# The partner-row transfers of the rotary embedding are begun by ScalarE instead of the sync engine

## The chip, the cores and the metric

The kernel runs on one core of one Trainium2 chip. The metric is the device time of one execution in microseconds (us). Engines are named as the profile names them: PE is TensorE (its matmuls; PEld its weight loads), DVE is VectorE, ACT is ScalarE, POOL is GpSimd, and SP is the sync engine, which does nothing here but start transfers (SPq is its queue).

## The reference

Two transformer blocks run one after the other on one sequence of 256 tokens with 1024 channels, all in float32. Each block has two layers. Cut to what matters here:

```
# first block, per layer
x = x + 0.5 * swiglu(rms_norm(x), w_gu, w_down)
x = x + hybrid_mixer(rms_norm(x))            # mixer1 below
x = x + 0.5 * swiglu(rms_norm(x), w_gu, w_down)

def hybrid_mixer(h):
    u, va, q, k, v, qi, ki, wi, g_a, g_b = split(h @ w_in)
    y_a = gmlp_spatial(u, va) @ w_pa
    q, k, qi, ki = rope(q), rope(k), rope(qi), rope(ki)
    # per query: the 64 keys with the highest index score, then attention on them
    score = sum_heads(relu(qi . ki) * wi);  selected = top_k(score, 64)
    y_b = attention(q, k, v, selected) @ w_pb
    return (sigmoid(g_a) * y_a + sigmoid(g_b) * y_b) @ w_out

def rope(x):            # per head; x1 and x2 are the two halves of the rotated channels
    return concat(x1 * cos - x2 * sin, x2 * cos + x1 * sin)

# second block, per layer
x = x + rms_norm(hybrid_mixer_2(rms_norm(x)))   # mixer2: gated delta rule beside dilated attention, rope on 16 of 64 channels
x = x + rms_norm(conv_glu(rms_norm(x)))
```

## The kernel before, in words

Channels lie on the 128 partitions and the 256 tokens along the free axis. A projection is computed in chunks of 128 output channels. Each chunk needs one weight slab of 128x1024, loaded from memory by SP into a tile `wraw` (four buffers). A float32 product is made of three passes on reduced-precision operands: ACT copies the slab rounded into `whi` (line 239, reported as L180), DVE subtracts to get the rest `wlo` (line 240, reported as L197), and PE then runs 24 matmuls for a chunk (`mm3`, L253). Slabs are rounded ahead, with four buffers each of `whi` and `wlo`. The sums land in three PSUM banks with the tag `mm`; small products use five banks with the tag `sm`.

Rotary embedding of a chunk is `rotated` (lines 585 to 596). DVE writes the chunk times the cosines (`m1`) and times the sines (`m2`) into a tile `rm` (two buffers), which also frees the PSUM bank. The two halves of a head lie on different partitions, and engines work partition by partition, so the sine products must be moved to the partner rows: four small transfers copy row groups of `m2` to `m2s` (L593; 32 rows of 256 numbers each in mixer1, 8 rows each in mixer2). POOL then adds `m1` and `m2s`. The buffers of `rm` and `m2s` (tiles `rm2s`, two buffers, and `pm2s`, one for each chunk of a pair) come free with this addition.

In `mixer1` (lines 708 to 852, twice per execution) 12 chunks are rotated: four `qi`, four `q`, four `k`. The single index key `ki` is rotated by lines 751 to 761 in the same way: two transfers of 32 rows (`km2s`, L758), an addition on DVE, and a third transfer that copies the 64 rows of `ki` to the other 64 partitions (L761), because the score matmuls (L686) use both halves. DVE then finds the 64 best keys by eight rounds of `max` and `match_replace` for each of two query blocks (L697, L699), while PE goes on with `va`, `v`, `q` and `k`. After the last `k` chunk the attention starts: scores (L615), exponentials on ACT (tile `as`), a scaling on POOL, transposes on PE (L638). Between these steps PE works through the gate projections in a fixed order (`pump`, with the amounts in `FILL1`).

In `mixer2` (lines 859 to 1071, twice per execution) four pairs of chunks are rotated (`Q`, `K`, `K`, `Q` in the order string), eight transfers for a pair. They lie beside the delta rule, whose triangular inverse (`inverse`, lines 1218 to 1310) is a serial chain of six levels: PE multiplies (L1257), DVE writes `Tf`, PE multiplies (L1267), ACT copies the result into `XTf`, PE transposes (L1276), ACT copies into `X`, and the next level begins. PE's order in mixer2 is written out by hand, with chunks of projections between the steps of the chain.

Each engine works through its instructions in order. The order is set when the program is built, by a scheduler that uses estimated durations of all instructions; inside `manual_schedule` the named engines keep the order in which the code is written. A transfer is an instruction of the engine that begins it: it waits for the data and the buffers that it needs, and what stands behind it on that engine waits with it. The transfers of the program share eight completion semaphores in turn, so that a transfer also waits for the earlier transfer on its semaphore. Before the change, all transfers of loads, partner rows and results stand on SP in one row.

Of the kernel before, what the change touches and what calls it, by code (L numbers as in the profile page):

```python
# [87 lines left out]
class Kernel:  # L88
# [496 lines left out]
    def rotated(self, pool, ps, cs, tag, swaps, m2s):  # L585

        nc = self.nc
        m = pool.tile([P, 2, T], F32, name="rm", tag="ct", bufs=2)
        m1, m2 = m[:, 0, :], m[:, 1, :]
        self.tt(m1, ps, cs[0])  # L590
        self.tt(m2, ps, cs[1])
        for to, frm, n in swaps:
            nc.sync.dma_start(m2s[to:to + n, :], m2[frm:frm + n, :])  # L593
        o = pool.tile([P, T], F32, name=tag, tag="rope", bufs=8)
        self.turned = self.tt(o, m1, m2s, OP.add, nc.gpsimd)
        return o
# [111 lines left out]
    def mixer1(self, l, vec):  # L708
        nc, I = self.nc, self.I
# [17 lines left out]
        with mp as mp:  # L727
# [26 lines left out]
            m2 = mp.tile([64, T], F32, name="km2")  # L754
            self.tt(m2, ps[:64, :], cs[1][:64, :])
            m2s = mp.tile([64, T], F32, name="km2s")
            for to, frm, n in swaps[:2]:
                nc.sync.dma_start(m2s[to:to + n, :], m2[frm:frm + n, :])  # L758
            ki = mp.tile([P, T], F32, name="ki")
            self.tt(ki[:64, :], m1, m2s, OP.add)  # L760
            nc.sync.dma_start(ki[64:, :], ki[:64, :])  # L761
            wi = mp.tile([72, T], F32, name="wi")
            self.tt(wi[64:, :], ps[64:, :], rb[64:72, :])
            ps = self.bank([P, 2, 8], "sm")
# [18 lines left out]
            for b, ps in enumerate(self.token_layout(I["w_in_va"][l], hs)):  # L783
# [8 lines left out]
                n = gv  # L792
# [739 lines left out]
```

## Time and profile before

| what | us |
|---|---|
| three runs, lowest / median / highest | 1924.41 / 1927.37 / 1934.48 |
| the profiled execution: its own time | 1928.9 |
| its span in the trace | 1927.2 |
| PE busy | 1857.0 (96%) |
| DVE busy | 1344.8 (70%) |
| ACT busy | 992.5 (51%) |
| POOL busy | 328.5 (17%) |

Busy time does not include instructions that begin transfers, so the table says nothing of what SP does. The share of busy time is a mean over stages with different limits. PE is idle for 70.2 us of the span, and most of that lies in the two mixers. A mixer1 starts at about 200 and at about 760 us, a mixer2 at about 1135 and at about 1560 us.

### The profile page before, as it was taken

The page shows a single profiled execution, that of the slowest core. Times are in us where ns is not written, and L with a number is a line of the kernel's source. Part 1 is how long each engine was busy: PE and PEld are TensorE (multiplying, and loading weights), DVE is VectorE, ACT ScalarE, POOL GpSimd, SP SyncE. Part 2 cuts the span into 40 slices and gives each one's busy share as a digit, 9 for nine tenths or more (in the row PEclk, how much of TensorE's full clock was granted, in tenths as well). Part 3 has the DMA queues.
Part 4 walks back from the last instruction along what each step waited for, and adds up shares of the span by engine and source line. Part 5 has one row for each costly group of instructions (what it writes and reads, how often), then busy time and mean ns, then how long its engine had stood idle before and what let it go on. Part 6 is the DMA issues. An engine that isn't in the chain of part 4 may idle for free. (4 is left out here: it accounts for less than half of the span.)

```text
span 1927.2 us, 38950 instructions
## 1 busy us (share of the span) xinstructions
PE 1857.0 (96%) x15468; PEld 1801.7 (93%) x15468; DVE 1344.8 (70%) x2318; ACT 992.5 (51%) x1698; POOL 328.5 (17%) x332
## 2 busy tenths in 40 slices
PE   9999989999999999999999998988999998989998
PEld 8999989999999999889999998968999998779998
DVE  6665696876656665886866659555997586558973
ACT  5444436554444544446544545535775564356762
POOL 1001131100010001220100123223231233132311
PEclk8999999999999999999999999999999999999999
DMA  7666654666666666564666653213566543135663
GB/s 232 187 182 185 205 153 149 192 188 186 183 189 191 192 186 204 164 188 130 205 192 186 181 167 123 95 59 102 186 196 185 156 132 98 57 115 168 197 185 108
DMA packets 102503, 317.10 MB, mean 165 GB/s; under 512 B 13361, under 2 KB 20913, under 8 KB 102321
## 3 DMA queue, kind: packets, MB, share of 16 engines
q1 hardware_dynamic: 102320, 314.61, 53.3%
q8 instruction: 121, 1.98, 0.4%
q14 instruction: 62, 0.50, 0.1%
HBM read 309.58 MB, written 1.05 MB: 161 GB/s over the span
## 5 line engine op out<-in xcount | busy, mean ns | idle before, releaser
L253 PE MATMUL mm<-h,whi 128*128 128x256 f32 x6048 | 1078.4, 281 | 17.2 <-DVE rm L197 8.4
L197 DVE TENSOR_TENSOR wlo<-wraw,whi 128x1024 fp32r<-128x1024 f32 (+2 forms) x611 | 716.2, 1174 | 357.9 <-ACT whi L180 355.8
L253 PEld LDWEIGHTS mm<-h,whi 128*128 128x128 f32 x6048 | 931.0, 190 | 24.3 <-ACT h L180 7.1
L180 ACT ACTIVATE whi<-wraw 128x1024 fp32r<-128x1024 f32 (+2 forms) x611 | 614.8, 1008 | 626.3 <-issue 286.5
L253 PE MATMUL mm<-h,wlo 128*128 128x256 f32 (+1 forms) x3024 | 728.3, 281 | 8.2 <-DVE wlo L197 8.0
L253 PEld LDWEIGHTS mm<-h,wlo 128*128 128x128 f32 (+1 forms) x3024 | 573.2, 190 | 11.0 <-DVE wlo L197 9.8
L253 PE MATMUL mm<-hid,whi 128*128 128x256 f32 x2112 | 374.1, 279 | 0.0
L253 PEld LDWEIGHTS mm<-hid,whi 128*128 128x128 f32 x2112 | 322.9, 188 | 0.0
L253 PE MATMUL mm<-hid,wlo 128*128 128x256 f32 x1056 | 255.1, 279 | 0.0
L253 PEld LDWEIGHTS mm<-hid,wlo 128*128 128x128 f32 x1056 | 198.1, 188 | 0.0
L197 POOL TENSOR_TENSOR ssum<-sq 128x256 f32<-128x256 f32 x19 | 23.4, 1232 | 674.2 <-ACT sq L180 674.2
L197 DVE TENSOR_TENSOR t<-mm,rb 128x512 f32<-128x512 f32 x132 | 90.7, 688 | 16.1 <-PE mm L253 7.7
L197 POOL TENSOR_TENSOR hid<-p,hid 128x256 fp32r<-128x256 f32 x44 | 63.9, 1453 | 179.6 <-ACT hid L180 149.8
L200 DVE SCALAR_TENSOR_TENSOR y<-t,vec,y 128x255 f32<-128x255 f32 (+1 forms) x176 | 91.7, 574 | 0.0
L197 POOL TENSOR_TENSOR ssum<-ssum,sq 128x256 f32<-128x256 f32 x50 | 54.9, 1097 | 204.2 <-ACT sq L180 178.8
L180 ACT ACTIVATE hid<-p 128x256 fp32r<-128x256 f32 x132 | 53.1, 402 | 5.7 <-DVE p L197 5.5
L180 ACT ACTIVATE y<-t,vec 128x256 f32<-128x256 f32 x88 | 47.7, 592 | 9.0 <-DVE t L197 8.8
L253 PE MATMUL mm<-zh,whi 128*128 128x256 f32 x256 | 45.4, 280 | 1.7 <-ACT zh L180 1.7
L200 DVE SCALAR_TENSOR_TENSOR h<-x,vec,h 128x256 fp32r<-128x256 f32 x72 | 41.1, 579 | 6.0 <-ACT h L180 5.1
L197 POOL TENSOR_TENSOR as<-as,ast 128x512 f32<-128x512 f32 (+1 forms) x32 | 26.1, 829 | 93.6 <-DVE ast L627 80.0
L253 PEld LDWEIGHTS mm<-zh,whi 128*128 128x128 f32 x256 | 39.0, 188 | 2.5 <-ACT zh L180 2.5
L573 PE MATMUL mm<-whi,h 128*128 128x512 f32 x96 | 39.6, 412 | 0.0
(294 smaller groups left out, 1899.2 us busy)
## 6 DMA issues: line engine op xcount, KB each, us to landing
wraw<-ffn_gu_in SPq DMA_DIRECT2D x175, 512.0 KB
wraw<-w_in_a_in SPq DMA_DIRECT2D x112, 512.0 KB
wraw<-up_in SPq DMA_DIRECT2D x88, 512.0 KB
wraw<-ffn_down_in SPq DMA_DIRECT2D x64, 512.0 KB
wraw<-down_in SPq DMA_DIRECT2D x32, 512.0 KB
wraw<-ffn_down_in SPq DMA_DIRECT2D x32, 384.0 KB
wraw<-w_in_v_in SPq DMA_DIRECT2D x16, 512.0 KB
wraw<-w_out_in SPq DMA_DIRECT2D x16, 512.0 KB
```

The lines of the kernel that those rows point to most:

```text
L180: return self.nc.scalar.activation(out, in_, func, **k)
L197: return (eng or self.nc.vector).tensor_tensor(out, a, b, op=op)
L200: return self.nc.vector.scalar_tensor_tensor(out, a, s, b, op0=op0, op1=op1)
L253: mm = lambda a, b, **f: self.nc.tensor.matmul(ps, a, b, skip_group_check=shared, **f)
L573: mm(ps[b], hs[k][:, 0, t], hi[:, w], start=k == 0, stop=False)
```

## The change

Three calls in two functions begin their transfer on ACT (`nc.scalar`) instead of SP (`nc.sync`). Data, shapes, buffers and arithmetic stay as they are.

```
 def rotated(self, pool, ps, cs, tag, swaps, m2s):
         for to, frm, n in swaps:
-            nc.sync.dma_start(m2s[to:to + n, :], m2[frm:frm + n, :])
+            nc.scalar.dma_start(m2s[to:to + n, :], m2[frm:frm + n, :])
...
 def mixer1(self, l, vec):
             for to, frm, n in swaps[:2]:
-                nc.sync.dma_start(m2s[to:to + n, :], m2[frm:frm + n, :])
+                nc.scalar.dma_start(m2s[to:to + n, :], m2[frm:frm + n, :])
             ki = mp.tile([P, T], F32, name="ki")
             self.tt(ki[:64, :], m1, m2s, OP.add)
-            nc.sync.dma_start(ki[64:, :], ki[:64, :])
+            nc.scalar.dma_start(ki[64:, :], ki[:64, :])
```

This moves 166 transfers: 2 x 48 `rm2s`, 2 x 2 `km2s` and 2 x 1 `ki` in mixer1, and 2 x 32 `pm2s` in mixer2. Since the scheduler sees other durations, it also orders other instructions anew in the mixers. Three places follow. A row is a run of like instructions, with its count behind an x.

ACT in the first mixer1, from the first rounding after `rb` (the row factors of the norm) to the first `rl` (rectified index scores); `gu` is a GELU of a `u` chunk. Before:

```order
L180 ACTIVATE whi<-wraw 128x1024 x4
L180 ACT_TABLE_LOAD
L180 ACTIVATE gu<-ut 128x256 x2
L180 ACTIVATE whi<-wraw 128x1024
L180 ACTIVATE gu<-ut 128x256
L180 ACTIVATE rl<-sm 128x2x128
L180 ACTIVATE whi<-wraw 128x1024 x2
```

With the change:

```order
L180 ACTIVATE whi<-wraw 128x1024
L593 DMA rm2s<-rm 32x256 x8
L180 ACTIVATE whi<-wraw 128x1024 x2
L593 DMA rm2s<-rm 32x256 x4
L758 DMA km2s<-km_2712 32x256
L593 DMA rm2s<-rm 32x256 x4
L758 DMA km2s<-km_2712 32x256
L180 ACT_TABLE_LOAD
L180 ACTIVATE gu<-ut 128x256 x2
L180 ACTIVATE whi<-wraw 128x1024 x4
L180 ACTIVATE gu<-ut 128x256
L761 DMA ki<-ki 64x256
```

Eighteen small transfers now stand among the roundings, and the copy of `ki` stands behind four roundings and three GELUs.

ACT in the first mixer1, from the last `ya` (the high part of a gMLP output) to the first exponentials of the attention (`as`). Before:

```order
L180 ACTIVATE ya<-gm_3221 128x256
L180 ACTIVATE whi<-wraw 128x1024 x5
L180 ACT_TABLE_LOAD
L180 ACTIVATE as,ast<-as,ast 128x256 x4
L180 ACTIVATE whi<-wraw 128x1024 x2
```

With the change:

```order
L180 ACTIVATE ya<-gm_3221 128x256
L593 DMA rm2s<-rm 32x256 x6
L180 ACTIVATE whi<-wraw 128x1024 x2
L593 DMA rm2s<-rm 32x256 x4
L180 ACTIVATE whi<-wraw 128x1024
L593 DMA rm2s<-rm 32x256 x8
L180 ACTIVATE whi<-wraw 128x1024 x2
L593 DMA rm2s<-rm 32x256 x4
L180 ACT_TABLE_LOAD
L180 ACTIVATE as,ast<-as,ast 128x256 x2
L180 ACTIVATE whi<-wraw 128x1024 x2
L180 ACTIVATE as,ast<-as,ast 128x256 x2
```

The same five roundings stand ahead of the table load, with 22 transfers among them; the last four, those of the last `k` chunk, stand directly ahead of the table load, and two roundings now split the four exponentials.

ACT in the first mixer2, from the last `vT` chunk's SiLU to level 1 of the inverse, as the difference (with `vec` for the taps of the convolution, `qT` a chunk of the delta rule's queries):

```order
-L180 ACTIVATE whi<-wraw 128x1024 x3
-L180 ACTIVATE XTf<-sm 64x4x64 x4
-L180 ACTIVATE whi<-wraw 128x1024
+L180 ACTIVATE whi<-wraw 128x1024
+L593 DMA pm2s_14549<-rm 8x256 x4
+L593 DMA pm2s_14551<-rm 8x256 x4
+L593 DMA pm2s_14549<-rm 8x256 x4
+L593 DMA pm2s_14551<-rm 8x256 x4
 L180 ACTIVATE XTf<-sm 64x4x64 x4
 L180 ACTIVATE qT<-ct,vec_2412 128x256 x2
+L180 ACTIVATE whi<-wraw 128x1024 x2
```

The sixteen transfers of the first `Q` pair and the first `K` pair now stand in one row ahead of the four `XTf` copies of level 0, and two roundings moved behind these. A third burst of eight (the second `K` pair) stands directly ahead of the four `XTf` copies of level 3, and a fourth (the second `Q` pair) ahead of the squares of the first delta output.

## Rows read from the trace of the kernel before

**Rows 1.** The page, part 1: busy time, share of the span, instructions.

```profile
PE 1857.0 (96%) x15468; PEld 1801.7 (93%) x15468; DVE 1344.8 (70%) x2318; ACT 992.5 (51%) x1698; POOL 328.5 (17%) x332
```

**Rows 2.** Busy time by stretch: mixer1's parts (830: second layer), then mixer2.

```profile
core 0: us, PE busy (x) PEld busy (x) DVE busy (x) ACT busy (x) POOL busy (x), PEclk, DMA share, GB/s
205.00:228.00 23.00, 23.00 (x196) 22.59 (x195) 11.93 (x24) 8.25 (x10) 4.44 (x6) 1.00 0.51 171
228.00:262.00 34.00, 32.36 (x183) 26.61 (x181) 31.77 (x64) 16.78 (x24) 7.65 (x6) 1.00 0.59 186
262.00:293.00 31.00, 26.80 (x216) 26.21 (x216) 28.20 (x62) 10.71 (x13) 9.08 (x10) 0.94 0.59 185
830.00:862.00 32.00, 27.78 (x235) 26.47 (x235) 26.66 (x67) 15.53 (x30) 9.73 (x12) 1.00 0.64 200
1190.00:1262.00 72.00, 64.58 (x559) 61.22 (x557) 44.09 (x93) 33.37 (x79) 20.14 (x24) 0.95 0.23 73
```

**Rows 3.** Waits of PE, 200 to 300: us in total, times, longest.

```profile
PE mm L253 <- DVE rm L197: 4.2, 2, 2.6
```

**Rows 4.** The tile rm2s: transfer instructions, duration in ns min/median/max.

```profile
L593 SPq DMA_DIRECT2D rm2s<-rm x96: 507/588/1567, 210.5 to 851.4; - x96
```

**Rows 5.** SP in order of time: start, us, operation; the q and k chunks.

```profile
266.48 2.43 SPq L593 DMA_DIRECT2D rm2s<-rm  x4
...
278.70 1.47 SPq L215 DMA_DIRECT2D wraw<-w_in_a_in  x3
280.27 6.36 SPq L593 DMA_DIRECT2D rm2s<-rm  x8
```

**Rows 6.** POOL and PE in order of time, k chunks (idle before, releaser).

```profile
287.01 0.72 POOL L197 TENSOR_TENSOR k<-rm,rm2s 128x256 f32<-128x256 f32 x1 [6.32 <-DMA rm2s<-rm]
...
288.67 0.36 PE L253 MATMUL mm<-h,whi 128*128 128x256 f32 x1 [2.64 <-DVE rm L197]
```

**Rows 7.** SP, then PE: the last km2s, the copy of ki and its first use.

```profile
222.64 0.59 SPq L758 DMA_DIRECT2D km2s<-km  x1
...
225.18 0.52 SPq L761 DMA_DIRECT2D ki<-ki  x1
...
226.98 0.71 PE L686 MATMUL sm<-ki,qi 64*128 64x128 f32 x4
```

**Rows 8.** ACT in order of time, both ends of the q and k chunks.

```profile
265.37 0.42 ACT L180 ACTIVATE ya<-gm 128x256 fp32r<-128x256 f32 x1 [2.12 <-DVE gm L197]
...
294.54 1.07 ACT L180 ACTIVATE whi<-wraw 128x1024 fp32r<-128x1024 f32 x1 [7.27 <-PE mm L253]
295.62 1.28 ACT L180 ACT_TABLE_LOAD   x1
296.92 0.51 ACT L180 ACTIVATE as<-as,ast 128x256 f32<-128x256 f32 x1
```

**Rows 9.** POOL, then PE: first scaled probabilities, first transposes; first scores.

```profile
298.29 2.04 POOL L197 TENSOR_TENSOR as<-as,ast 128x512 f32<-128x512 f32 x2 [2.57 <-DVE ast L627]
...
300.12 0.60 PE L638 MATMUL sm<-ident,as 128*128 128x128 f32 x4
```

**Rows 10.** SP, ACT, PE in mixer2: bursts beside levels 0, 1 and 3.

```profile
1207.16 5.41 SPq L593 DMA_DIRECT2D pm2s<-rm  x8
...
1226.02 5.41 SPq L593 DMA_DIRECT2D pm2s<-rm  x8
...
1207.06 0.78 ACT L180 ACTIVATE XTf<-sm 64x256 f32<-64x256 f32 x2 [1.84 <-PE sm L1269]
...
1225.94 1.06 ACT L180 ACTIVATE whi<-wraw 128x1024 fp32r<-128x1024 f32 x1
1230.42 1.69 ACT L180 ACTIVATE XTf<-sm 64x256 f32<-64x256 f32 x4 [3.42 <-PE sm L1267]
...
1213.15 1.95 PE L1267 MATMUL sm<-XTf,Tf 128*128 128x128 f32 x16
...
1231.66 1.16 PE L1276 MATMUL sm<-ident,XTf 128*128 128x128 f32 x8
```

More of the change, by code (lines that the diff above doesn't have):

```diff
@@ L592, in rotated @@
         for to, frm, n in swaps:
-            nc.sync.dma_start(m2s[to:to + n, :], m2[frm:frm + n, :])
+            nc.scalar.dma_start(m2s[to:to + n, :], m2[frm:frm + n, :])
         o = pool.tile([P, T], F32, name=tag, tag="rope", bufs=8)
@@ L757, in mixer1 @@
             for to, frm, n in swaps[:2]:
-                nc.sync.dma_start(m2s[to:to + n, :], m2[frm:frm + n, :])
+                nc.scalar.dma_start(m2s[to:to + n, :], m2[frm:frm + n, :])
             ki = mp.tile([P, T], F32, name="ki")
             self.tt(ki[:64, :], m1, m2s, OP.add)
-            nc.sync.dma_start(ki[64:, :], ki[:64, :])
+            nc.scalar.dma_start(ki[64:, :], ki[:64, :])
             wi = mp.tile([72, T], F32, name="wi")
```

## The prediction

> **What bounds the kernel now.** The page's busy times come first: PE is busy 1857.0 of 1927.2 us [rows 1]. A change that touches no matmul can give back only PE's idle time, and it costs what it adds to that. So the question is where PE idles near the moved transfers, and for whom it waits there. The view of busy time by stretch answers the first part [rows 2]. In mixer1 PE has no gap while the qi chunks are rotated (205 to 228), 1.6 us in the top-k stretch (228 to 262) and 4.2 us in the stretch of the q and k chunks (262 to 293; again 4.2 in the second layer). In these last two stretches DVE is nearly full too, 31.8 of 34 and 28.2 of 31 us, while ACT is busy for 16.8 and 10.7. In mixer2, 1190 to 1262, PE idles 7.4 us.
>
> The list of PE's waits says for whom: in the first mixer1, 4.2 us go to DVE's `rm` [rows 3], the instruction that frees a PSUM bank. `rm` is late because its two buffers come free only when POOL has added the partner rows. The rows of SP and POOL show it: the first k chunk's transfers are begun at 280.27, right behind three weight slabs, and POOL can add only at 287.01, after 6.32 us of idleness put down to these transfers; PE stands for 2.64 us until 288.67 [rows 5, 6]. So the small transfers do sit on PE's path there, but only there.
>
> **The price of a transfer on ACT.** A transfer keeps SP's queue 588 ns (median; 507 at least) [rows 4], and four take 2.43 us, 0.61 each with the gaps [rows 5]. No row shows ACT beginning one. From above I take SP's 0.61 with nothing beside it; from below, zero, since an activation that runs may cover an instruction that only begins a transfer. I take 0.61, because it is the same instruction, but let the first one or two of a burst run under the activation ahead of them. Each mixer1 moves 48 + 2 + 1 = 51 transfers, 31 us of ACT's queue, and each mixer2 moves 32, 19.5 us. Whatever stands behind one on ACT waits also for what the transfer waits for: DVE's `rm`, POOL's freeing of the buffer, and the earlier transfer on its semaphore.
>
> **Part a, the qi chunks and ki (each mixer1).** SP began the copy of ki at 225.18, and PE used it at 226.98, 1.8 us later [rows 7]. With the change the copy stands on ACT behind 18 transfers, a table load, four roundings and three GELUs. The last transfer before the table load, a `km2s`, was begun by SP from 222.64 to 223.23 [rows 7]; I assume the same on ACT. Then the load 1.28, two GELUs 0.8, four roundings 4 x 1.0, a third GELU 0.4: ki's copy begins at about 229.8 and can be used at 231.6, against 226.98. In its new order PE has about one more chunk ahead of these scores, 24 matmuls at 23.00 / 196 = 0.117 us, 2.8 us [rows 2], so until about 230; it stands some 1.5 us. The first va rounding moves back with the same row of instructions; I put that at 1 us for PE, 2.5 together. A stretch follows in which DVE sets the pace, and a PE that arrives late there idles less. I take half, +1.2; bounds 0 and +2.5.
>
> **Part b, the q and k chunks (each mixer1).** The gain: SP no longer holds weights back behind `rm`, and the small transfers no longer queue behind slabs on SP's queue. At most it is the 4.2 us of idle PE, and in the first layer another 31 x 0.06 = 1.9 us of granted clock lost (0.94 there, 1.00 in the second) [rows 2]. But DVE, 28.2 of 31 us busy, leaves 2.8 us before it is the limit itself. The cost: ACT's 10.7 busy us and 32 x 0.61 = 19.5 make 30.2 of 31. ACT goes from an idle engine to a full one; if its waits for `rm` come on top, roundings are late. By SP's price and with nothing overlapped I bound that at +2.0. I take -2; bounds -4.2 (-6.1 in the first layer) and +2.0.
>
> **Part c, the start of attention (each mixer1).** ACT's last rounding before it began at 294.54 after a wait for PE; table load and exponentials follow at 295.62 and 296.92 [rows 8]. With the change the last k chunk's four transfers stand between: 4 x 0.61 = 2.4 us, 1.4 if they begin under the rounding. The first half of POOL's scaling ended at about 299.3, PE's transposes began at 300.12 [rows 9]: 0.8 us of slack. So 0.6 to 1.6 us reach PE; I take +0.8, bounds 0 and +1.6.
>
> **Part d, the inverse in mixer2 (each mixer2).** Three bursts stand directly ahead of copies that the chain needs or its squares. The first K pair's burst ran on SP from 1207.16 for 5.41 us, to 1212.6. On ACT the four `XTf` copies of level 0 come behind it: 4 x 0.39 = 1.6, done at 1214.1 instead of 1207.84. PE needs them at 1213.15 [rows 10], so +0.9. The second K pair's burst, 1226.02 to 1231.4 on SP, delays `XTf` of level 3 from 1230.42 to 1231.4, +1.0 (2.0 if it begins only when the rounding has ended at 1227.0); PE's transposes at 1231.66 move with it. The fourth burst delays squares of the first half's output by about 1.1 us; the second half ends later anyway, so I count 0.3. The first Q pair's burst is covered by the wait for level 0. Sum +2.2; bounds 0 and +4.0 by these rows, and 5.4 + 5.4 + 1.1 = 11.9 if the bursts land in full on the chain. Nothing comes back here: none of PE's waits in mixer2 ends on a `pm2s` transfer.
>
> **The sum.** Each mixer1: 1.2 - 2 + 0.8 = 0. Each mixer2: +2.2. Against the profiled execution's 1928.9 us (1927.2 of span, and 1.5 above the median of 1927.37) the forecast is 1928.9 + 2 x 0 + 2 x 2.2 = 1933.3 us, own range 1924 to 1943.
>
> **The rivals.** *ACT is held (slower).* ACT begins one transfer at a time, nothing of it under an activation. Then a, b and c stand at their upper bounds, 2.5 + 2.0 + 1.6 = 6.1 in each mixer1, and d at 4.0: 1928.9 + 2 x 10.1 = 1949.1. It decides from the point at which ACT's price reaches SP's 0.59 without overlap. For it: ACT would be full in the q and k stretch. Against it: ACT idled 7.27 us just before 294.54 [rows 8].
>
> *The small transfers get through (faster).* Taken out of SP's queue, they land soon after they begin, as the copy of ki did in 1.8 us [rows 7], instead of some 4 to 6 us when slabs stand ahead [rows 5, 6]. Then all of PE's waits on `rm` go, and ACT hides the rest: -4.2 in each mixer1 and -1.9 of clock, nothing else: 1928.9 - 10.3 = 1918.6. For it: rows 5 and 6. Against it: DVE is the next limit. The Trainium skill, "DMA: Bandwidth & Descriptors", section "Queues, rings and completion order", supports it: SP and ACT each own a row of rings, and each DMA engine takes turns between the rows that have work.
>
> *The weights do not come free (the change does not do what it says).* The semaphores still go round over both queues, so that SP's loads wait for earlier small transfers which ACT has not begun, and these share the DMA engines with slabs as before. Then b is 0 and the rest stays: 1928.9 + 2 x 2.0 + 2 x 2.2 = 1937.3. For it: the second k chunk's transfers took longer to begin than the usual 2.43 for four (eight took 6.36 us [rows 5]), so such waits exist already. The Trainium skill speaks for it too, in the same page's section "Issuing engines are not separate DMA queues": transfers from all engines run on the same 16 DMA engines, and issuing from several saves only the issuing time. By that rule alone the time would be 1937.3. Rows 6 do not tell the two apart, since all transfers of this trace come from SP.
>
> **How the numbers follow.** Chances: forecast 0.50, ACT held 0.24, transfers get through 0.10, weights not free 0.16. The range 1920 to 1949 leaves out about half of the slower rival and most of the faster one, some 0.19 in all. What a measurement can tell from no change is about 0.5%, 9.6 us: faster means below 1917.7, slower above 1937.0. Faster: nearly half of the second rival and a little of the forecast's low side, 0.06. Slower: nearly all of the first rival, half of the third and 0.05 of the forecast, 0.36. Same: 0.58.
>
> **What would show it.** In the changed trace: the transfers of `rm2s` on ACT's queue near 0.6 us each; PE's waits on `rm` in the q and k stretches down from 4.2 us; a PE wait before the index scores (L686) of 1 to 3 us; `XTf` of levels 0 and 3 starting right behind a burst. The forecast is wrong if ACT's price is far from 0.6, if PE's idle time in mixer2 grows by more than 4 us a layer, or if stretches without moved transfers change.

## The result and the profile after

The changed kernel takes 1940.04 us (median of 19 runs, 1932.66 to 1949.94) against 1926.12 us before (19 runs of the same series, 1916.65 to 1935.96). The ratio is 1.0070, 95% interval 1.0057 to 1.0084: 11 to 16 us slower, beyond the 0.5% that a measurement tells from no change. The prediction was 1933.3 in a range from 1920 to 1949, with 0.58 on "same". By its own bounds (slower above 1937.0) the outcome is "slower", to which it gave 0.36.

The profiled execution of after has a span of 1942.5 us. Its lines that answer to the rows of before are these. First the busy times [rows 1]:

```profile
PE 1867.2 (96%) x15468; PEld 1808.4 (93%) x15468; DVE 1341.7 (69%) x2318; ACT 991.3 (51%) x1698; POOL 337.8 (17%) x332
```

Next, from the list of PE's waits over the whole span (us in total, times, longest), the lines that the change bears on:

```profile
PE sm L1267 <- ACT XTf L180: 8.3, 2, 4.4
PE mm L253 <- DVE rm L197: 7.6, 9, 1.7
...
PE sm L686 <- DVE ki L197: 3.6, 2, 2.2
...
PE sm L1276 <- ACT XTf L180: 1.8, 3, 0.8
```

The waits on `rm`, which the change could have removed, are still there: 4.8 of these 7.6 us lie in the first mixer1 (3.8 in the stretch of the q and k chunks, 1.0 new among the qi chunks), against 4.2 before, all of them in the q and k chunks [rows 3]. The other three lines show PE waiting for ACT's copies in mixer2 (L1267, L1276) and for `ki` in mixer1 (L686).

Then line 593, the transfers themselves (duration in ns min/median/max), and who waited for them (us, times). It answers to [rows 4]:

```profile
L593 ACTq DMA_DIRECT2D rm2s<-rm x96: 514/602/1400, 208.2 to 853.5; - x96
...
L593 ACTq DMA_DIRECT2D pm2s<-rm x64: 631/632/1182, 1198.5 to 1674.5; - x64
...
  POOL qi L197: 35.6, 6
  ACT whi L180: 29.9, 7
  POOL rope L197: 27.2, 12
```

A transfer costs ACT what it cost SP, 0.6 us. New is the second waiter: ACT's own roundings, 29.9 us.

**Where the 13.9 us lie.** A stage is counted from the write of its row factor `rb` to the next one's. The experiments below leave one mixer or the other as it was, so that their profiles give several executions of each stage with its old code, and chance can be told from effect. For mixer2's first layer the three changed stages (205.7 to 206.5) touch the longest of the seven old ones.

| stage length, us | old code, mean (range) | all on ACT, mean | difference |
|---|---|---|---|
| mixer1, start to PE's first attention transposes (both layers) | 90.9 (89.1 to 93.1; 14 stages) | 93.4 (6 stages) | +2.5 |
| mixer2, first layer | 202.7 (200.8 to 205.8; 7) | 206.1 (3) | +3.4 |
| mixer2, second layer | 196.6 (196.0 to 197.2; 7) | 203.0 (3) | +6.4 |

The sum is 2 x 2.5 + 3.4 + 6.4 = 14.8 us, within the measured 11 to 16. So the loss is in mixer1 and mixer2, where transfers were moved.

### The profile page after: what moved, and what is told of

Its sections match the earlier page's. It is cut to its first block, busy times and chain, and to the rows that moved or that the text cites. A ratio compares the mean times of both kernels' runs of the same rounds, so it can differ in the third digit from the quotient of the medians.

```text
span 1942.5 us, 38929 instructions
## 1 busy us (share of the span) xinstructions
PE 1867.2 (96%) x15468; PEld 1808.4 (93%) x15468; DVE 1341.7 (69%) x2318; ACT 991.3 (51%) x1698; POOL 337.8 (17%) x332
## 3 DMA queue, kind: packets, MB, share of 16 engines
q1 hardware_dynamic: 96336, 310.67, 52.2%
## 5 line engine op out<-in xcount | busy, mean ns | idle before, releaser
L197 DVE TENSOR_TENSOR t<-mm,rb 128x512 f32<-128x512 f32 x132 | 90.6, 687 | 14.4 <-PE mm L253 7.5
L197 POOL TENSOR_TENSOR hid<-p,hid 128x256 fp32r<-128x256 f32 x44 | 62.1, 1410 | 184.2 <-ACT hid L180 155.4
L197 POOL TENSOR_TENSOR ssum<-ssum,sq 128x256 f32<-128x256 f32 x50 | 54.9, 1098 | 203.7 <-ACT sq L180 178.2
L180 ACT ACTIVATE XTf<-sm 64x256 f32<-64x256 f32 (+1 forms) x48 | 17.3, 360 | 58.0 <-DMA pm2s<-rm 26.0
L197 DVE TENSOR_TENSOR rm<-mm,cosr 128x256 f32<-128x256 f32 x40 | 16.6, 419 | 39.2 <-POOL qi L197 10.8
```

Source lines behind the costliest of these rows:

```text
L180: return self.nc.scalar.activation(out, in_, func, **k)
L197: return (eng or self.nc.vector).tensor_tensor(out, a, b, op=op)
```

## The experiments

Each timed kernel ran in turns with the kernel before. "Before" in the ratios is that kernel on the same chips.

**One mixer at a time.** The helper gets the queue as an argument; mixer1 passes ACT and mixer2 SP, or the other way round.

```diff
-            nc.scalar.dma_start(m2s[to:to + n, :], m2[frm:frm + n, :])
+            queue.dma_start(m2s[to:to + n, :], m2[frm:frm + n, :])
```

> Only mixer1's transfers (rm2s, km2s and the copy of ki) are begun by ACT; mixer2's pm2s stay on SP. The changed kernel is 13.9 us slower than the kernel before (1940.0 against 1926.1). Theory 'held copies': most of the loss sits in mixer2, where ACT's XTf copies stand behind K bursts; mixer1 costs 1.7 us a layer (PE's first transposes of attention come 1.7 us late in both layers of the changed trace), so 1926.1 + 3.4 = 1929.5, and mixer2's stages last as before. Rival 'price by number': every transfer on ACT costs the same, 13.9 us / 166 transfers = 0.084 us; 102 of them are here, so 1934.7. Rival 'slow matmuls': the 4.9 us that the first conv_glu lost in the changed trace, where PE did 215 matmuls in 25 us instead of 223, come from the moved transfers too, in whichever mixer; then this kernel's conv_glu also runs at 215.

Measured: 1934.12 us (12 runs), ratio 1.0043 (1.0021 to 1.0064), 4 to 12 us.

> Only mixer2's pm2s transfers are begun by ACT; mixer1's stay on SP. Theory 'held copies': 3.0 to 6.1 us a layer, as the two layers of the changed trace show, so 1926.1 + 9 = 1935 (1932 to 1938), with PE's wait before L1267 on XTf of 4 us a layer and its wait before L1276 of 0.8. Rival 'price by number': 64 x 0.084 = 5.4 us, 1931.5. Both mixers' losses should add up to 13.9 if nothing couples them.

Measured: 1937.83 us (10 runs), ratio 1.0062 (1.0035 to 1.0088), 7 to 17 us, with PE's wait before L1267 on `XTf` at 4.7 us in the first layer. Both halves lose. Their medians add up to more than 13.9, but their intervals include a pair that adds up to it. Mixer1 costs more than the 3.4 us expected; the price by number fits it (8.3 against 8.5) but not mixer2 (11.9 against 5.4). The next runs separate places from numbers.

**The two halves of mixer1.** First only the q and k chunks on ACT, then only qi, `km2s` and `ki`:

```diff
-                    out.append(self.rotated(mp, chunk(i0 + i), cs, tag, swaps, m2s))
+                    out.append(self.rotated(mp, chunk(i0 + i), cs, tag, swaps, m2s, nc.scalar if i0 else nc.sync))
```

> Only the transfers of mixer1's q and k chunks (L593 in the second call of rope_chunks) are begun by ACT; qi, km2s, the copy of ki and mixer2's pm2s stay on SP. Theory 'held copies': the wait of PE before L686 on ki is gone; what is left is the start of attention (+0.7 us a layer) against a gain of 0.6 to 1 us a layer in the stretch before it, so 1925 to 1927. The prediction's term b (-2 a layer) with term c (+0.8): 1926.1 - 2.4 = 1923.7. Rival 'price by number': 64 x 0.084 = +5.4, 1931.5.

Measured: 1934.18 us, 1.0030 (1.0008 to 1.0052), above the theory's 1925 to 1927, while its two mixer1 stages were 0.45 us shorter and 0.53 longer than in the first profile of before. Its two conv_glu stages, which no edit touches, were 5.0 and 3.8 us longer. So it was run again:

> The kernel with only the q and k chunks on ACT, once more: it was timed at 1.0030 (1.0008 to 1.0052), while its mixer1 stages took as long as before and its conv_glu stages, whose code is the same, 5.0 and 3.9 us longer. If the loss is in conv_glu by chance (two equal kernels differ there too), this time comes out within 0.2% of before, 1925 to 1930. If the transfers themselves cost 5.8 us, 1933 to 1935 again, with the loss in mixer1.

Measured: 1926.49 us, 1.0008 (0.9983 to 1.0033); mixer1 +0.30 and +0.53 us. The 64 transfers of q and k bring nothing. What they cost is small: about half a us at most shows in a mixer1 stage, and what both series allow is 2 to 6 us over the execution (1.0008 to 1.0033).

> The other half of mixer1: qi's transfers, km2s and the copy of ki are begun by ACT; the q and k chunks and mixer2 stay on SP. From the traces so far, PE's first transposes of attention stand 90.9 us after the start of mixer1 in 14 stages whose mixer1 is that of before (89.1 to 93.1), 93.1 in four stages with all of it on ACT, and 91.1 in two with only q and k on ACT. Theory 'late ki': this half carries the loss of mixer1, 2.2 to 2.5 us a layer, so PE reads ki first 20.2 to 21.2 us after the stage's start instead of 18.6, and the time is 1927 + 4.7 = 1931.7. Rival 'price by number': 38 transfers, 3.2 us, 1930; and the wait on ki would not matter. Rival 'given back' (DVE sets the pace of the stretch that follows): 1927.

Measured: 1934.28 us, 1.0044 (1.0026 to 1.0063), with PE's first read of `ki` 20.8 and 20.5 us after the start of mixer1 (18.5 to 18.8 where SP begins the transfers). The 38 transfers of this half carry as much as the whole of mixer1 (1.0043); "price by number" and "given back" fall. Its last step takes `km2s` and `ki` off ACT again and leaves qi there:

```diff
             for to, frm, n in swaps[:2]:
-                nc.scalar.dma_start(m2s[to:to + n, :], m2[frm:frm + n, :])
+                nc.sync.dma_start(m2s[to:to + n, :], m2[frm:frm + n, :])
...
-            nc.scalar.dma_start(ki[64:, :], ki[:64, :])
+            nc.sync.dma_start(ki[64:, :], ki[:64, :])
```

> Only the qi chunks' 16 transfers a layer are begun by ACT; km2s and the copy of ki are back on SP, where they now stand between va's weight slabs. Theory 'late ki because its km2s and its copy stand behind qi's burst on ACT': PE reads ki first 18.6 us after the stage's start again, the cost goes: 1926 to 1928. Rival 'roundings are late behind qi's burst' (the first transposes of wi stood 1 us later in the changed trace already): 1 to 2 us a layer stay, 1929 to 1931, with ki read at 19.6 or later.

Measured: 1927.82 us, 1.0013 (0.9994 to 1.0031). SP's row of `km2s` and PE's first scores in the first layer, whose mixer1 starts at 205.49:

```profile
215.90 1.46 SPq L758 DMA_DIRECT2D km2s<-km  x2
...
223.15 0.71 PE L686 MATMUL sm<-ki,qi 64*128 64x128 f32 x4
```

Both `km2s` transfers are begun from 10.4 us after the start of the stage on, where SP's second one came after 14.4 us before and ACT's after 16.6, and `ki` is read after 17.7 us, before even the kernel before. Most of the time is back: 1.0013 against 1.0044. So `km2s` and the copy of `ki` behind qi's transfers on ACT cost the larger part. But a rest of 1 to 2 us a layer, as the rival said, shows in the trace and is within the interval, though `ki` is early: PE's first transposes of `wi` are 0.5 to 0.9 us late, its last matmuls on `ws` and `gv` (the gMLP's spatial product, which closes this stretch) come 54.2 and 53.8 us after the start (54.4 and 54.1 with `ki` on ACT too, 51.7 to 53.0 with the old code), and the first attention transposes after 93.6 and 90.9. What this rest is was not tested; qi's transfers on ACT are what is left of the change there.

**The two kinds of pair in mixer2.** Only the Q pairs on ACT, then only the K pairs (mixer1 on SP in both):

```diff
-                        out.append(self.rotated(mp, ps[:, s, :], cs, "rope", swaps, m2s[s]))
+                        out.append(self.rotated(mp, ps[:, s, :], cs, "rope", swaps, m2s[s], nc.scalar if out is q else nc.sync))
```

> In mixer2 only the Q pairs' transfers are begun by ACT; K pairs and all of mixer1 stay on SP. Theory 'burst in front of copies': a burst costs PE only where XTf or X copies that the inverse needs next stand behind it; the Q bursts have free time behind them (the first Q burst cost nothing at level 0 when the K burst was moved away), so 0 to 1 us a layer, 1926 to 1930, and mixer2's stages within 1 us of before. Rival 'late landing': the Q pair's rows land some 5 us after they are begun because SP's slabs run freely, POOL's addition and what stands behind it on POOL are late, and the cost stays at 2 us or more a layer. Rival 'price by number': 32 x 0.19 = 6 us, from the 11.9 us that 64 transfers in mixer2 cost.

Measured: 1928.47 us, 1.0001 (0.9978 to 1.0024).

> In mixer2 only the K pairs' transfers are begun by ACT; Q pairs and all of mixer1 stay on SP. In its order three of level 0's eight XTf copies more than before stand ahead of the first K burst, the other five behind it. Theory 'burst in front of copies': the burst starts when it started on SP in the kernel before (its rm is ready then, because the Q pair lands early again) and is over 5.4 us later, just before PE needs the copies; by the working of the prediction +0.9 or less for the first and +1.0 for the second, 1.0 to 2.0 us a layer, 1928 to 1930. Rival 'the K burst by itself': 4 to 6 us a layer as with all of mixer2's transfers on ACT, 1935 to 1938; the first Q pair's landing would then be without a part in it.

Measured: 1936.86 us, 1.0057 (1.0035 to 1.0078). The same number of transfers, 32 each, costs nothing in one place and about 11 us in the other: "price by number" falls in mixer2 too. The K pairs carry the loss, and more of it than the 1 to 2 us a layer of the prediction's working. The profile shows less than the median: it is that of the fastest of the ten runs (1930.45 us), and its mixer2 stages are 2.9 and 3.9 us longer than the means with the old code.

**The same number in another place.** The K pairs' transfers and additions are kept back and written behind the `XTf` copies of the level at which they fall:

```diff
+        if held is None:
+            partner()
+        else:
+            held.append(partner)
...
                 for b in range(2):
                     step(lev, b)
+                while i == 1 and k.held:
+                    with k.tc.issue_after(self.copied.ins):
+                        k.held.pop(0)()
                 k.pump(WAIT["lev%d" % i])
```

> As the kernel with only mixer2's transfers on ACT, but each K pair's transfers and POOL's additions behind them are written after the XTf copies of the inverse's level (0 and 3) that they stood in front of. Same number of transfers on ACT. Theory 'held copies': PE's wait on XTf before the first L1267 goes, and the cost falls from 9 us to 2 (1926 to 1929). Rival 'price by number' and rival 'late landing' (the transfers land late because SP's weight slabs are no longer held back behind them, and whoever needs the rotated chunks is late): nothing comes back, within 2 us of the kernel with mixer2's transfers on ACT.

Measured: 1945.26 us, 1.0100 (1.0065 to 1.0134): slower still, against the theory's 1926 to 1929. Its trace says why. ACT's rows in the first layer, then PE's row behind them:

```profile
1205.95 1.59 ACT L180 ACTIVATE XTf<-sm 64x256 f32<-64x256 f32 x4 [9.22 <-DMA pm2s<-rm]
1207.71 5.41 ACTq L596 DMA_DIRECT2D pm2s<-rm  x8
...
1233.36 4.85 ACTq L596 DMA_DIRECT2D pm2s<-rm  x7
1238.31 1.56 ACT L180 ACTIVATE X<-sm 64x256 f32<-64x256 f32 x4 [5.08 <-DMA pm2s<-rm]
...
1239.13 3.67 PE L1265 MATMUL sm<-X,LT 128*128 128x64 f32 x16 [3.93 <-ACT X L180]
```

The first burst now starts behind level 0's copies. At level 2 PE is 1.2 and 1.8 us late in the two layers, counted from the start of the stage against the mean of the seven stages with the old code, instead of 4.4 and 4.8 with the burst ahead of the copies. The second burst, moved from before the `XTf` copies of level 3 to behind them, now stands before that level's `X` copies, and its 5 us hold PE for 3.93. By the end of the inverse the layers are 7.8 and 8.4 us late. So the theory was right on the first burst and too narrow: the `X` copies, which the inverse needs next, cost as `XTf` did. "Price by number" falls, and so does "late landing" as the only cause, since with the same number of transfers each layer gained 3 us at the first burst's new place and lost 5.6 more at the second's.

**Weights held back again.** One more small transfer per chunk on SP, into a tile nobody reads, where SP's transfers stood before:

```diff
+        if extra is not None:
+            to, frm, n = swaps[0]
+            self.nc.sync.dma_start(extra[to:to + n, :], m2[frm:frm + n, :])
         for to, frm, n in swaps:
             queue.dma_start(m2s[to:to + n, :], m2[frm:frm + n, :])
```

> As the kernel with mixer2's transfers on ACT, with one more small transfer per rotated chunk on SP, into a tile that nobody reads, at the place where SP's transfers stood before. It holds SP's next weight slab back until rm is there, as before; ACT's burst is unchanged. Theory 'late landing': the first Q pair lands 2 us after it is begun instead of 5, POOL adds earlier, the K burst ends earlier, PE's wait for XTf before the first L1267 falls from 4.7 to under 2 us, and the time from 1937.8 to 1932 or less. Rival 'the K burst by itself': PE's waits stay, 1936 to 1940.

Measured: 1939.01 us, 1.0061 (1.0036 to 1.0086), as without the extra transfers. POOL's rows at the first Q pair, and PE's at level 1:

```profile
1190.17 0.73 POOL L197 TENSOR_TENSOR dM<-levels,cM 128x256 f32<-128x256 f32 x1 [6.21 <-DVE Tf L197]
1190.86 0.74 POOL L197 TENSOR_TENSOR rope<-rm,pm2s 128x256 f32<-128x256 f32 x1
...
1200.31 3.78 PE L1271 MATMUL sm<-XTf,Tf 128*128 128x128 f32 x16 [4.00 <-ACT XTf L180]
```

POOL no longer waits for the landing; it adds as soon as it gets there. But in this kernel's order it gets there late, behind a `dM` that waits for DVE. So this is no clean test of what the landing cost; it shows that early landing alone does not give the time back, because the K burst in front of the copies then ends no earlier (64.1 and 62.1 us after the start of the stage, against 63.2 and 61.7 without the extra transfers).

**Controls.** The kernel before and the changed kernel once more:

> The kernel before, unchanged, as a measure of what two equal kernels differ by, and for a second profile of it. Expected: ratio 1.000 within 0.002. In the kernel before's first profile both conv_glu stages ran at 223 matmuls in 25 us and took 193.6 and 183.8 us; in other profiles one or both took some 4 to 5 us more. If the matmul rate is a matter of the execution, this profile may show either; if it is a matter of the moved transfers, both stages take 193.6 and 183.8 again.

Measured: 1925.26 us, 0.9994 (0.9971 to 1.0016).

> The changed kernel, for a second profile. If the first conv_glu's loss of 4.9 us comes with the change, it shows again; if the matmul rate is a matter of the execution, either 193 or 198 us. Mixer1 1.5 to 3 us longer than before in each layer and mixer2 3 to 6, in either case.

Measured: one time of 1941.76 us; mixer1 2.6 and 2.7, mixer2 2.2 and 6.0 us longer than in the first profile of before; first conv_glu 193.2 us. The 4.9 us that this stage lost in the first profile of after do not come with the change; that also answers the rival "slow matmuls".

No run kept the transfers on SP and changed only the order of the other instructions, which the scheduler makes anew with every edit. What the new order alone costs is not known.

## Why the prediction came out as it did

The sign of the forecast was right and the size was a third of it: +4.4 us forecast, +13.9 measured, between the third rival's 1937.3 and the first's 1949.1. That the time lies in the stated range is no merit of the working: the range reached up to the slowest rival. By the stage averages, over both layers, a came out 2.8 us above its term, b 3.0 above, c 1.0 below and d 5.4 above; the sum of 10.2 is near the 9.5 us between the changes forecast and measured. By its own steps:

**The price, right.** 0.61 us a transfer was taken; the medians are 602 and 632 ns. That the first of a burst runs under the activation ahead was right too, and understated, as the copy of `ki` below shows.

**Part a (+1.2), mis-sized: +2.6 a layer, just above its upper bound.** Counted from the start of the stage, PE's last matmul on `ws` and `gv` (the end of the stretch that a speaks of) comes after 54.9 us on average against 52.2 with the old code. In two of the six changed stages the granted clock fell to its lower level, 1.2 GHz, shortly behind the wait on `ki` (0.97 on average over the stretch, 1.00 in the others); the other four come at 54.4. The rows of the first layer, in the order SP, ACT, POOL, DVE, PE:

```profile
209.64 18.84 SPq L215 DMA_DIRECT2D wraw<-w_in_va_in  x4
...
208.19 5.18 ACTq L593 DMA_DIRECT2D rm2s<-rm  x8
213.47 2.01 ACT L180 ACTIVATE whi<-wraw 128x1024 fp32r<-128x1024 f32 x2 [5.45 <-DMA rm2s<-rm]
...
222.60 0.60 ACTq L758 DMA_DIRECT2D km2s<-km  x1
...
227.02 0.52 ACTq L761 DMA_DIRECT2D ki<-ki  x1
...
214.45 1.43 POOL L197 TENSOR_TENSOR qi<-rm,rm2s 128x256 f32<-128x256 f32 x2 [9.27 <-DMA rm2s<-rm]
...
215.22 0.42 DVE L197 TENSOR_TENSOR rm<-mm,cosr 128x256 f32<-128x256 f32 x1 [5.60 <-POOL qi L197]
...
226.02 0.97 DVE L197 TENSOR_TENSOR ki<-km,km2s 64x256 f32<-64x256 f32 x1 [0.54 <-DMA km2s<-km]
...
216.12 0.35 PE L253 MATMUL mm<-h,whi 128*128 128x256 f32 x1 [0.99 <-DVE rm L197]
...
227.13 0.68 PE L686 MATMUL sm<-ki,qi 64*128 64x128 f32 x4 [2.18 <-DVE ki L197]
```

Before, DVE's addition for `ki`, and PE's only longer wait of this stretch (us in total, times, longest):

```profile
224.60 0.44 DVE L197 TENSOR_TENSOR ki<-km,km2s 64x256 f32<-64x256 f32 x1 [0.62 <-DMA km2s<-km]
...
PE sm L806 <- POOL gv L197: 1.5, 1, 1.5
```

This mixer1 starts at 205.98, that of before at 208.29. Counted from there, the first qi transfer begins at 2.2 us in both. But SP, whose slabs for va stood behind all of these transfers before, now starts them from 209.64 on, and POOL can add only at 8.5, after 9.27 us of idleness that ends on the transfers; before it added at 6.1. That the slabs delay the landing fits these rows; no run held them back in mixer1. DVE needs that buffer for the third chunk's `rm` (5.60 us of idleness, and 0.99 for PE behind it), and the last `km2s` goes out at 16.6 instead of 14.4 [rows 7]. It also lands later: DVE's addition follows 3.4 us after it is begun instead of 2.0, and takes 0.97 us instead of 0.44. So `ki` is ready after 21.0 us instead of 16.8, and PE reads it after 21.2 instead of 18.7. The step that failed is "I assume the same on ACT" for the last `km2s`: the clock time is nearly the same, 222.60, but the stage started 2.3 us earlier. The copy of `ki`, on which the working turned, was not what PE waited for: the first scores read the half that DVE writes. The copy went out at 227.02, 2.8 us earlier than predicted, although two roundings and a GELU stand ahead of it in ACT's order (two of the roundings began at 227.05): ACT's queue runs ahead of its engine here. Of what this stretch was to give back, PE's wait of 1.5 us on `gv` before the last matmuls is gone; against the two new waits, 0.99 and 2.18 us, that was not half.

**Part b (-2), wrong: -0.5 at most.** From that matmul to the first attention scores PE takes 30.6 us instead of 31.1, and 31.0 with the q and k chunks alone on ACT. SP is free, and its weights run on in one unbroken row, but POOL waits for the k chunks' rows as before [rows 5, 6]:

```profile
240.38 57.31 SPq L215 DMA_DIRECT2D wraw<-w_in_a_in  x17
...
287.32 0.72 POOL L197 TENSOR_TENSOR k<-rm,rm2s 128x256 f32<-128x256 f32 x1 [3.69 <-DMA rm2s<-rm]
291.68 0.72 POOL L197 TENSOR_TENSOR k<-rm,rm2s 128x256 f32<-128x256 f32 x1 [3.64 <-DMA rm2s<-rm]
```

One wait of 6.32 us has become two of 3.7, and PE's stall on `rm` several short ones. That is nearly the third rival's "b is 0". The rows fit the second of its two reasons, that the small transfers share the DMA engines with slabs, which nothing holds back any more; no run held the slabs back in this stretch. The Trainium skill, "DMA: Bandwidth & Descriptors", section "Issuing engines are not separate DMA queues", says that transfers from all engines run on the same 16 DMA engines and that issuing from several saves only the issuing time; the rows of the q and k chunks agree, with 1.0030 and 1.0008 for that part alone. The forecast left this reason at 0.16 because the trace of before could not show it. The faster rival falls by the same rows.

**Part c (+0.8), right in sign and smaller.** From PE's first attention scores to its first transposes there are 7.6 us in the 14 stages with old code and 7.5 to 8.2 in the six with all transfers on ACT, 7.9 on average: +0.3.

**Part d (+2.2), mis-sized: +3.4 and +6.4.** ACT, POOL and PE in the first layer:

```profile
1198.47 14.61 ACTq L593 DMA_DIRECT2D pm2s<-rm  x16
1213.13 1.58 ACT L180 ACTIVATE XTf<-sm 64x256 f32<-64x256 f32 x4 [15.11 <-DVE ct L197]
1214.74 0.91 ACT L180 ACTIVATE qT<-ct,vec 128x256 f32<-128x256 f32 x2
1215.56 1.99 ACT L180 ACTIVATE whi<-wraw 128x1024 fp32r<-128x1024 f32 x2
1217.57 1.59 ACT L180 ACTIVATE XTf<-sm 64x256 f32<-64x256 f32 x4
...
1229.67 5.58 ACTq L593 DMA_DIRECT2D pm2s<-rm  x8
1235.35 1.58 ACT L180 ACTIVATE XTf<-sm 64x256 f32<-64x256 f32 x4 [4.78 <-DMA pm2s<-rm]
...
1206.07 0.74 POOL L197 TENSOR_TENSOR rope<-rm,pm2s 128x256 f32<-128x256 f32 x1 [7.86 <-DMA pm2s<-rm]
...
1213.97 3.78 PE L1267 MATMUL sm<-XTf,Tf 128*128 128x128 f32 x16 [4.43 <-ACT XTf L180]
1218.62 1.54 PE L1276 MATMUL sm<-ident,XTf 128*128 128x128 f32 x8
...
1236.18 1.46 PE L1276 MATMUL sm<-ident,XTf 128*128 128x128 f32 x8 [0.80 <-ACT XTf L180]
```

Then PE's wait and the matmuls behind it, as busy time by stretch (us, then PE, PEld, DVE, ACT, POOL with counts, granted clock, DMA share, GB/s):

```profile
1209.50:1213.97 4.47, 0.04 (x2) 0.01 (x1) 2.45 (x6) 0.79 (x3) 2.13 (x3) 0.87 0.06 13
1213.97:1217.75 3.78, 3.78 (x17) 3.78 (x18) 2.47 (x5) 3.71 (x7) 0.73 (x1) 0.50 0.00 0
```

For the second K burst the working holds: +1.0 forecast, PE's wait is 0.80 and its delay grows by 1.0 in both layers. For the first the end of level 0's copies was well forecast (1214.1; 1214.7, in a stage that starts 1.0 later), though the sixteen transfers take 14.61 us instead of 16 x 0.63 = 10.1: POOL waits 7.86 us for the first Q pair's rows. Against the mean of the seven stages with the old code PE's L1267 starts 1.5 us late in the first layer and 2.1 in the second. What the working left out comes next: PE had idled for 4.43 us, the granted clock fell to 0.50, its lower level of 1.2 GHz, and the same 16 matmuls took 3.78 us instead of 1.95 [rows 10]. This is so in all six stages with mixer2's transfers on ACT: a wait of 3.2 to 4.7 us, then 3.2 to 3.8 us for these matmuls, against 1.95 to 2.04 in the 14 stages with the old code. At level 1's L1276 PE is therefore 3.7 and 4.2 us late. ACT's queue does not explain this: two `qT` steps and two roundings, 2.9 us, now run ahead of level 1's copies (1217.57), but L1276 shows no wait on these copies. So the mis-sized term is "+0.9" for the first K burst: it counted how late the copies come, and put the clock that PE loses while it waits for them at nothing. The runs with the K pairs alone (1.0057), the Q pairs alone (1.0001) and the burst moved behind the copies (no such wait, 2.04 us for the 16 matmuls) bear out the place. In the one profile with the K pairs alone PE waits on these copies in pieces of 1.8 us at most, the clock stays at 1.00 there, and PE is 2.9 and 2.7 us late at the end of the inverse; no run separates the clock's part from the wait's.

At the end of the inverse the two layers are alike, 4.9 and 5.2 us late. Behind it the first layer wins 1.5 back and the second loses 1.2 more; why is open. The Q pairs alone lengthened the second layer by 3.7 us in their one profile, with nothing in their time.

The measurement lies nearest to the third rival's 1937.3, but as a change, 13.9 us, it is about midway between that rival's 8.4 and the first's 20.2. The third rival's "b is 0" came true, and its reason may have a part in a as well. The first rival, "ACT is held", holds where a burst stood in front of work on the chain (a, d) and not where ACT was said to be fullest (b, c). Of the signs named in advance, the price, the wait on `ki` of 1 to 3 us and the copies right behind a burst came true; the fall of PE's waits on `rm` did not.

## What to carry to other kernels

A transfer that is moved to a compute engine costs that engine the time to begin it and the wait for its data: price it by what stands next in that engine's order, copies for the bottleneck first, and count what the wait does to the bottleneck's clock: behind 4.43 us of idleness 16 matmuls took 3.78 us instead of 1.95. A queue that is relieved does not rest: without its waits for small transfers SP began its weight slabs at once, and the rows landed no sooner, among qi's chunks later. Between equal numbers of transfers the place decided: over both layers 32 in front of the inverse's copies cost 11 us, 32 elsewhere in the same stage nothing.

## What the runs showed that was not expected

PE's matmul rate in dense stages has two levels with the granted clock at 1.00 (its upper level, 2.4 GHz) in both. Busy time of the same 50 us of the first conv_glu (us, then PE, PEld, DVE, ACT, POOL with counts, granted clock, DMA share, GB/s), in the two profiles of the changed kernel:

```profile
1407.42:1457.42 50.00, 50.00 (x427) 50.00 (x426) 47.38 (x72) 33.92 (x54) 12.89 (x9) 1.00 0.60 188
```

```profile
1410.55:1460.55 50.00, 50.00 (x443) 50.00 (x443) 49.69 (x76) 35.78 (x56) 14.30 (x9) 1.00 0.62 198
```

443 against 427 matmuls are 113 and 117 ns each, and the stage took 193.2 or 198.5 us. The kernel before showed the same between its two profiles, in the second conv_glu (183.8 and 187.7 us) and in a feed-forward stage (187.9 and 183.5). What chooses the level was not found; PE has no idle time in either. The difference in one such stage is about a third of the effect studied here, so single profiles were compared stage by stage, and totals by medians.
